# Last step of a blocked state-space scan in four pieces of eight channel groups, with the output matmuls one piece behind

## The chip, the cores and the metric

The kernel runs on one core of a Trainium2 chip. The metric is the device time of one execution in microseconds (us). Five engines matter here: TensorE (PE in the rows, with its weight loads as PEld), VectorE (DVE), ScalarE (ACT), GpSimd (POOL) and SyncE (SP), whose queue issues nearly all transfers.

## The reference, cut to what matters

One inference step of a two-layer backbone. Each layer runs four mixers side by side on 640 tokens (128 prompt tokens and 512 latent tokens): three kinds of attention and one state-space mixer. The change touches only the state-space mixer, which for each of two directions, 32 channel groups and 64 complex states computes a linear recurrence over time and then maps the states to outputs:

```python
bu = jnp.einsum('btgn,gpn->btgp', u, bbar)            # input to the states
_, hs = lax.associative_scan(_lin_combine, (a, bu))   # h[t] = abar * h[t-1] + bu[t], complex
y = jnp.real(jnp.einsum('btgp,gnp->btgn', hs, cmat))  # outputs, per channel group
```

The gate and merge projections of the other branches (`h @ w_in`) have nothing to do with the scan, and the kernel uses them as filling.

## The kernel before, in words

Tokens are cut into 80 chunks of eight. The state at a chunk's edge is what the scan computes; inside a chunk everything is matmuls. The states lie in a tile `H` of 128 partitions by 82 slots by 64 columns: partitions 0 to 63 hold real parts and 64 to 127 imaginary parts of the 64 states, slots are chunk edges, and the 64 columns are 2 directions by 32 channel groups.

`ssm_scan` works on `H` with DVE alone. One complex multiply-add is the helper `madd` (five instructions, L595 to L599): two of 64 partitions each that fetch the imaginary parts for the real rows and the reverse, then three of all 128 partitions. It runs in three levels over blocks of eight chunks: a sequential pass inside blocks (seven steps, tiles `sc1v`, `sc2v`), a sequential pass over the blocks' ends (tiles `sc1c`, `sc2c`), and a last step that spreads the carry of each block to its seven inner slots. The last step is one `madd` per direction over 7 blocks by 7 slots by 32 groups (1568 elements a partition, tiles `sc1f`, `sc2f`), and a small one per direction for the prompt's second block (224 elements, `sc1g`, `sc2g`). The scheduler puts the small ones between the carry steps, since nothing holds them back.

`ssm_out` then makes the outputs in four pieces of eight groups. Each piece loads two tiles of constants (`M`, from `fd`, eight transfers, two buffers; `WY`, from `yd`, two transfers, four buffers) and has two halves; a half is four groups of three matmuls into one PSUM tile `sm` (L645 from `M`, L646 with `H` of direction 0, L647 with `H` of direction 1) and one eviction by ACT (L649).

PE's instructions stand in the order in which the code emits them. Other engines are ordered by a scheduler. Between the steps of the scan the code calls `fill(n)`, which emits the next n units of a queue of gate and merge projections; a unit is three matmuls of 320 columns (L152, L154, L156). So PE has work while DVE scans. The numbers of units are in the table `FILL`: 9 after each inner step, 4 after each carry step, 20 after each large last step, 4 after each small one, and 4 after the scan; one more follows each half of the outputs. After the scan and the outputs come transposes (L1413), GELU and the gated linear unit of the state-space branch, and then the attentions, which go on taking units from the same queue.

Of the kernel before, what the change touches and what calls it, by code (L numbers as in the profile page):

```python
# [15 lines left out]
ALU = mybir.AluOpType  # L16
AX = mybir.AxisListType

P = 128
# [20 lines left out]
GB = 2  # L40
QB, KB, VB, OB = 2, 3, 2, 2

FILL = {"a": 1, "s": 8, "t": 4, "e": 3, "m": 6, "ms": 6, "scan": (9, 4, 20), "l": (8, 8), "f": 0.7, "d": 8, "p": (3, 2), "g": 34}
HD_SCALE = 64 ** -0.5


# [9 lines left out]
def hybrid_kernel(ctx: ExitStack, tc: tile.TileContext, A, O, dbg=None):  # L56
    nc = tc.nc
    V, S, G, T = nc.vector, nc.scalar, nc.gpsimd, nc.tensor
# [12 lines left out]
    def taker(pool):  # L71
        def take(tag, shape, bufs=1, dt=F32):
            return pool.tile(shape, dt, tag=tag, name=nm(tag), bufs=bufs)
        return take
# [6 lines left out]
    def load(dst, src):  # L81
        nc.sync.dma_start(dst, src)
        return dst

    def dump(name, ap, l=None):
        if dbg is not None and f"{name}{l}" in dbg:
            nc.sync.dma_start(dbg[f"{name}{l}"], ap)
# [28 lines left out]
    def psum1():  # L116
        return ps.tile([P, 512], F32, tag="sm", name=nm("sm"), bufs=2)
# [40 lines left out]
    def fm_tile(src, mhi, mlo, nk=KD, eng=V):  # L158

        o = psum2()  # L160
        kc = min(nk, 4)
        for kq in range(nk // kc):
            w = w_chunk(src[kq], [P, kc, P], eng)
            for kk in range(kc):
                k = kq * kc + kk
                mm3([o[:, 0, 192:512], o[:, 1, 0:320]], w[0][:, kk], w[1][:, kk],
                    [mhi[:, k, 0:HF], mhi[:, k, HF:NT]], [mlo[:, k, 0:HF], mlo[:, k, HF:NT]], k == 0, k == nk - 1)
        return run2(o)[:, 192:832]
# [371 lines left out]
    def chunk_powers(l, at):  # L540

        A8, tm = at("A8p", [P, 8, 2, 64]), at("pwt", [P, 4, 64])
        V.tensor_copy(A8[:, 0], A8s[l])
        for n in (1, 2, 4):
            double(A8, n - 1, tm, n)
        V.tensor_scalar(A8[:, :, 1], A8[:, :, 1], sgn, None, op0=ALU.mult)
        return A8
# [31 lines left out]
        V.memset(H[:, 80, 32:64], 0.0)  # L579
        return U  # L580

    def hview(H, rows, d, off, *dims):

        b = H[rows, 1 + off:2 + off, 32 * d:32 * d + 1]
        slot, dg = H.ap[1][0], H.ap[2][0]
        return bass.AP(tensor=b.tensor, offset=b.offset, ap=[b.ap[0]] + [[32 * d_ * dg + s_ * slot, n] for d_, s_, n in dims] + [[dg, 32]])

    def ssm_scan(at, A8, H, final):

        all_, top, bot = slice(0, P), slice(0, 64), slice(64, P)  # L590

        def madd(ar, ai, src, dst, shape, t, nb=1):

            m, m2 = at("sc1" + t, shape, nb), at("sc2" + t, shape, nb)
            V.tensor_tensor(m2[top], ai[bot], src(bot), ALU.mult)  # L595
            V.tensor_tensor(m2[bot], ai[top], src(top), ALU.mult)  # L596
            V.tensor_tensor(m, ar, src(all_), ALU.mult)
            V.tensor_tensor(m2, m2, dst, ALU.add)
            V.tensor_tensor(dst, m, m2, ALU.add)  # L599

        def power(k, n=None):

            for ri in range(2):
                v = A8[:, k - 1, ri].rearrange("p (d g) -> p d g", d=2)
                yield v.unsqueeze(2).to_broadcast([P, 2, n, 32]) if n else v

        for i in range(7):
            ar, ai = power(1, 10)
            v = lambda f, b: (lambda r: hview(H, r, 0, f, (1, b - f, 2), (0, 8, 10)))
            madd(ar, ai, v(i, 7 - i), v(i + 1, 6 - i)(all_), [P, 2, 10, 32], "v")  # L610
            fill(FILL["scan"][0])
        for j in range(1, 8):

            n = 2 if j == 4 else None
            ar, ai = power(8, n)
            both = [(0, 40, 2)] if n else []
            v = lambda f, b: (lambda r: hview(H, r, 0, f, (1, b - f, 2), *both))
            madd(ar, ai, v(8 * j - 1, 64 - 8 * j), v(8 * j + 7, 56 - 8 * j)(all_), [P, 2, 2, 32] if n else [P, 2, 32], "c", 2)
            fill(FILL["scan"][1])
        ar, ai = power(1)  # L620
        madd(ar, ai, lambda r: hview(H, r, 0, 79, (1, -15, 2)), final.rearrange("p (d g) -> p d g", d=2), [P, 2, 32], "c", 2)
        for n in (7, 1):
            for d in range(2):

                sh = [P, n, 7, 32]
                f_, t_ = ((8, 7) if d == 0 else (1, 8)) if n == 7 else ((72, 71) if d == 0 else (65, 72))
                k = slice(0, 7) if d == 0 else slice(6, None, -1)
                ar, ai = (A8[:, k, ri, 32 * d:32 * d + 32].unsqueeze(1).to_broadcast(sh) for ri in range(2))
                madd(ar, ai, lambda r: hview(H, r, d, t_, (0, 8, n), (0, 0, 7)), hview(H, all_, d, f_, (0, 8, n), (0, 1, 7)), sh, "f" if n == 7 else "g")
                fill(FILL["scan"][2] if n == 7 else 4)  # L630

    def ssm_out(l, at, U, H, ysb):

        for gb in range(4):
            g0 = 8 * gb
            M = at("M", [P, 8, P], 2)
            for j in range(8):
                load(M[16 * j:16 * j + 16], fd[l][:, g0:g0 + 8, 16 * j:16 * j + P])
            Y = [load(at("WY", [P, 8, 8, 16], 4), yd[l][2 * gb + d][:, :, 1 - d:9 - d]) for d in range(2)]
            for q in range(2):  # L640
                py = psum1()
                for n in range(4):
                    g = 4 * q + n
                    o = py[0:80, P * n:P * n + P]
                    T.matmul(o, lhsT=U[:, g0 + g], rhs=M[:, g], start=True, stop=False)  # L645
                    T.matmul(o, lhsT=H[:, 1:81, g0 + g], rhs=Y[0][:, g], start=False, stop=False)  # L646
                    T.matmul(o, lhsT=H[:, 1:81, 32 + g0 + g], rhs=Y[1][:, g], start=False, stop=True)  # L647
                a = 16 * (g0 + 4 * q)
                S.activation(ysb[:, :, a:a + 64].rearrange("c i (g n) -> c g i n", g=4),  # L649
                             py[0:80].rearrange("c (g i n) -> c g i n", g=4, i=8), AF.Copy)  # L650
                fill(1)


    queue, owed, emitted, TAIL = [], [0], set(), object()

    def fill(n):

        owed[0] += n
        while owed[0] >= 1 and queue:
            try:  # L660
                next(queue[0])
                owed[0] -= 1
            except StopIteration:
                queue.pop(0)
        owed[0] %= 1
# [11 lines left out]
    def drain(*gens):  # L677
        for g in gens:
            for _ in g:
                pass  # L680
# [112 lines left out]
    def softmax(at, s, p_out, scale, total):  # L793

        mx = at("mx", [P, 2], 6)
        V.tensor_reduce(mx[:, 0:1], s, axis=AX.X, op=ALU.max, negate=True)  # L796
        if scale is None:
            S.activation(p_out, s, AF.Exp, bias=mx[:, 0:1], accum_out=total)
        else:
            V.tensor_tensor(mx[:, 1:2], mx[:, 0:1], scale, ALU.mult)  # L800
            S.activation(p_out, s, AF.Exp, bias=mx[:, 1:2], scale=scale, accum_out=total)
# [32 lines left out]
    def slot():  # L834

        due = [fn for n, fn in later if n == 0]
        later[:] = [(n - 1, fn) for n, fn in later if n > 0]
        for fn in due:
            fn()
# [4 lines left out]
    def p_t(at, p, pp, fl=1.0):  # L844

        out = []
        for k0, nk in ((0, 2), (2, 2), (4, 1)):
            if k0 == 4:
                fill(fl * 2)
                slot()  # L850
                fill(fl * (FILL["t"] - 2))
            pt = psum1()
# [11 lines left out]
            if w == 384:  # L864
                out.append((hi[:, 256:384], lo[:, 256:384]))
        fill(fl * FILL["e"])
        return out
# [14 lines left out]
    def attend64(at, passes, v, scale, o, row, total, done=None, fl=1.0):  # L882
# [12 lines left out]
        for half in range(2):  # L895
            p, pp = at("p", [P, 2, NT], PB), at("pp", [P, P], 2) if half else None
            for jj in range(2):
# [3 lines left out]
                if j == 3:  # L901
                    softmax(at, s[1], pp, scale(4), total[:, 4, row // 64:row // 64 + 1])
            fill(fl * FILL["a"])
            slot()
# [410 lines left out]
    for l in range(DEPTH):  # L1315
# [10 lines left out]
        for k in range(KD):  # L1326
            sh, sc = mods[l, 0], mods[l, 1]
            t = xat("ht", [P, NT], 2)
# [53 lines left out]
        at = taker(sp)  # L1382
# [13 lines left out]
        H, final = at("H", [P, 82, 64]), at("final", [P, 64])  # L1396
        A8 = chunk_powers(l, at)
        U = ssm_states(l, at, ucm, H, final)
        ssm_scan(at, A8, H, final)
        fill(4)  # L1400
        dump("H", H, l)
        ysb = at("cm", [80, 8, 512])
        ssm_out(l, at, U, H, ysb)
        dump("ysb", ysb, l)

        yh = at("U", [P, 4, NT])
# [38 lines left out]
        at = lambda tag, *a, takers=(taker(bp), taker(kp)): takers[tag in ("k", "q", "v")](tag, *a)  # L1445
# [8 lines left out]
        b = []  # L1454
# [22 lines left out]
        for d_ in range(KD):  # L1477
            bo = fm_tile(A["wbo"][l, 1, d_], *b, 4, G)
            t = load(xat("ht", [P, NT], 2), ttd[l][1][d_])
# [7 lines left out]
        for d_ in range(KD):  # L1487
            g = fm_tile(A["wout"][l, d_], mhi, mlo, KD, G)
# [184 lines left out]
```

## Time and profile before

| what | before |
|---|---|
| median of 3 runs | 2258.31 us (2257.4 to 2258.47) |
| the profiled execution's own time | 2259.87 us |
| its span, first to last instruction | 2258.1 us |
| PE busy | 2069.8 us, 92% |
| DVE busy | 1333.8 us, 59% |
| ACT busy | 965.6 us, 43% |
| POOL busy | 795.5 us, 35% |
| mean granted TensorE clock | 0.959 of full |

Times inside the trace count from the start of the span. The state-space mixer of layer 0 ends its scan near 467 us, that of layer 1 near 1567 us. A wait is the idle time of an engine in front of an instruction, put down to the instruction that released it.

### The profile page before, as it was taken

The numbers are of one execution on the slowest core, as the hardware profiler recorded it, in microseconds if no ns is written. First come the engines' busy times: TensorE is split into PE (matmuls) and PEld (weight loads), VectorE is DVE, ScalarE is ACT, GpSimd is POOL, SyncE is SP. The second block draws the span as 40 slices with busy tenths as digits, with TensorE's granted clock in tenths as the row PEclk, the third lists the DMA queues.
The fourth block names the chain that finished last, engine by engine and source line by source line (L and its number), as shares of the span: only waits on it lengthen the run. The fifth ranks groups of instructions, "written<-read, shape, count | busy, mean of one in ns | idle before, by whom it ended". The sixth has DMA issues, their size and how long they took to land. (4 is left out here: it accounts for less than half of the span.)

```text
span 2258.1 us, 38400 instructions
## 1 busy us (share of the span) xinstructions
PE 2069.8 (92%) x14389; PEld 1993.9 (88%) x14389; DVE 1333.8 (59%) x2461; ACT 965.6 (43%) x1972; POOL 795.5 (35%) x561
## 2 busy tenths in 40 slices
PE   5888899969999999998798999997899999999997
PEld 3787789969998899998787999997899899999997
DVE  7899372935544455664877774367445445566542
ACT  3342344324554455553233434341455455555332
POOL 1655432403311232345563364232142223234522
PEclk9889899989999999999898999998999999999998
DMA  7366675535555665666573577653474445666653
GB/s 253 101 233 212 202 268 160 154 76 187 177 155 158 189 198 167 183 197 194 178 258 116 150 246 240 206 186 88 120 242 135 147 134 156 185 187 188 203 156 112
DMA packets 240538, 400.62 MB, mean 177 GB/s; under 512 B 37536, under 2 KB 112288, under 8 KB 240352
## 3 DMA queue, kind: packets, MB, share of 16 engines
q1 hardware_dynamic: 226112, 372.14, 53.9%
q10 hardware_dynamic: 14240, 26.02, 3.1%
q8 instruction: 113, 1.85, 0.4%
q14 instruction: 73, 0.60, 0.1%
HBM read 279.68 MB, written 117.87 MB: 176 GB/s over the span
## 5 line engine op out<-in xcount | busy, mean ns | idle before, releaser
L135 POOL TENSOR_TENSOR flo<-fraw,fhi 128x512 fp32r<-128x512 f32 x304 | 436.2, 1439 | 937.9 <-ACT fhi L134 854.6
L152 PE MATMUL mm<-hhi,fhi 128*128 128x320 f32 x2048 | 669.9, 327 | 22.8 <-DVE gt L774 8.2
L156 PE MATMUL mm<-hhi,flo 128*128 128x320 f32 x2048 | 642.5, 314 | 4.3 <-POOL flo L135 4.3
L154 PE MATMUL mm<-hlo,fhi 128*128 128x320 f32 x2048 | 641.6, 313 | 0.0
L152 PEld LDWEIGHTS mm<-hhi,fhi 128*128 128x128 f32 x2048 | 394.7, 193 | 38.2 <-issue 7.6
L156 PEld LDWEIGHTS mm<-hhi,flo 128*128 128x128 f32 x2048 | 392.7, 192 | 5.4 <-POOL flo L135 5.4
L154 PEld LDWEIGHTS mm<-hlo,fhi 128*128 128x128 f32 x2048 | 394.5, 193 | 0.4
L134 ACT ACTIVATE fhi<-fraw 128x512 fp32r<-128x512 f32 x304 | 190.1, 628 | 128.6 <-PE mm L154 94.5
L135 DVE TENSOR_TENSOR ptl<-sm,pth 128x512 fp32r<-128x512 f32 (+1 forms) x240 | 142.2, 620 | 171.7 <-ACT pth L134 171.4
L796 DVE TENSOR_REDUCE mx<-s 128x1 f32<-128x640 f32 (+1 forms) x240 | 167.5, 714 | 112.3 <-PE s L829 57.7
L135 POOL TENSOR_TENSOR wlo<-wraw,whi 128x512 fp32r<-128x512 f32 (+1 forms) x80 | 114.6, 1436 | 231.4 <-ACT whi L134 224.7
L134 ACT ACTIVATE pth<-sm 128x512 fp32r<-128x512 f32 (+1 forms) x240 | 122.3, 543 | 163.5 <-PE sm L856 126.6
L829 PE MATMUL s<-k,q 128*128 128x384 f32 (+5 forms) x1008 | 158.4, 304 | 1.7 <-DMA q<-gqd 1.1
L829 PEld LDWEIGHTS s<-k,q 128*128 128x128 f32 (+1 forms) x1008 | 154.7, 189 | 2.5 <-issue 1.6
L152 PE MATMUL mm<-bh,fhi 128*128 128x320 f32 x384 | 126.4, 329 | 6.5 <-DVE gt L774 3.2
L134 ACT ACTIVATE whi<-wraw 128x512 fp32r<-128x512 f32 (+1 forms) x96 | 59.2, 618 | 170.7 <-PE s L154 90.6
L856 PE MATMUL sm<-ident,p 128*128 128x128 f32 x800 | 116.1, 274 | 5.3 <-DVE ptl L135 3.2
L879 PE MATMUL sm<-pth,v 128*128 128x256 f32 (+1 forms) x528 | 120.2, 282 | 0.0
L727 ACT ACTIVATE gt<-mm 128x320 f32<-128x320 f32 x192 | 82.9, 432 | 86.9 <-PE mm L156 84.9
L156 PE MATMUL mm<-bh,flo 128*128 128x320 f32 x384 | 119.5, 311 | 0.0
L154 PE MATMUL mm<-bl,fhi 128*128 128x320 f32 x384 | 119.3, 311 | 0.0
L879 PE MATMUL sm<-ptl,v 128*128 128x256 f32 (+1 forms) x440 | 112.5, 281 | 0.0
(418 smaller groups left out, 3995.6 us busy)
## 6 DMA issues: line engine op xcount, KB each, us to landing
fraw<-in_wmerge SPq DMA_DIRECT2D x128, 256.0 KB, 3.0
fraw<-in_wgate SPq DMA_DIRECT2D x64, 256.0 KB, 2.9
mgd<-gt SPq DMA_DIRECT2D x48, 320.0 KB, 2.9
fraw<-in_wbo SPq DMA_DIRECT2D x48, 256.0 KB, 2.9
k<-dkd SPq DMA_DIRECT2D x64, 192.0 KB, 4.1
gtd<-gt SPq DMA_DIRECT2D x32, 320.0 KB, 3.2
pv<-mgd SPq DMA_DIRECT2D x32, 320.0 KB, 3.7
pv<-brd SPq DMA_DIRECT2D x30, 320.0 KB, 3.7
```

The lines of the kernel that those rows point to most:

```text
L134: S.activation(hi, src, AF.Copy)
L135: eng.tensor_tensor(lo, src, f(hi), ALU.subtract)
L152: T.matmul(outs[i], lhsT=whi, rhs=mhis[i], start=first, stop=False)
L154: T.matmul(outs[i], lhsT=whi, rhs=mlos[i], start=False, stop=False)
L156: T.matmul(outs[i], lhsT=wlo, rhs=mhis[i], start=False, stop=last)
L727: S.activation(t[:, r[0]], r[1], AF.Tanh, scale=0.5)
L796: V.tensor_reduce(mx[:, 0:1], s, axis=AX.X, op=ALU.max, negate=True)
L829: T.matmul(o, lhsT=tok(q, t), rhs=k[:, a:b], start=i == 0, stop=i == n - 1)
L856: T.transpose(pt[:, a:a + P], p[:, jj, P * kt:P * kt + P], ident)
L879: T.matmul(o, lhsT=v, rhs=p_, start=n == 0, stop=n == len(todo) - 1)
```

## The change

The last step is turned round. First the two small steps of the prompt are emitted. Then the carries of the seven blocks (both directions, all groups) are copied once into a tile `sw` with real and imaginary parts exchanged, by two copies of 64 partitions. With that tile a multiply-add needs four instructions, all of 128 partitions. The last step is cut into four pieces of eight channel groups; a piece does both directions (2 times 4 instructions of 7 by 7 by 8, that is 392 elements). `ssm_scan` and `ssm_out` become generators, and the caller takes them in turn: after the second, third and fourth piece of the scan the outputs of the piece before it are emitted, and the last outputs follow the scan. The units of filling: 4 after each small step, 29 after the first piece, 5 after each of the other three.

```diff
-FILL = {..., "scan": (9, 4, 20), ...}
+FILL = {..., "scan": (9, 4, 29, 5), ...}
...
-        for n in (7, 1):
+
+        sw = at("sw", [P, 2, 7, 32])
+        for to, of in ((top, bot), (bot, top)):
+            V.tensor_copy(sw[to], hview(H, of, 0, 7, (1, 1, 2), (0, 8, 7)))
+        for d in range(2):
+            f_, t_ = (72, 71) if d == 0 else (65, 72)
+            ...
+            madd(ar, ai, lambda r: hview(H, r, d, t_, (0, 0, 7)), hview(H, all_, d, f_, (0, 1, 7)), [P, 7, 32], "g")
+            fill(4)
+        for g in range(0, 32, 8):
             for d in range(2):
-                sh = [P, n, 7, 32]
-                ...
-                madd(ar, ai, ..., sh, "f" if n == 7 else "g")
-                fill(FILL["scan"][2] if n == 7 else 4)
+                f_, t_ = (8, 7) if d == 0 else (1, 8)
+                sh = [P, 7, 7, 8]
+                ...
+                V.tensor_tensor(m2, ai, sw[:, d, :, g:g + 8].unsqueeze(2).to_broadcast(sh), ALU.mult)
+                V.tensor_tensor(m, ar, hview(H, all_, d, t_, (0, 8, 7), (0, 0, 7), g=g, ng=8), ALU.mult)
+                V.tensor_tensor(m2, dst_, m2, ALU.subtract)
+                V.tensor_tensor(dst_, m, m2, ALU.add)
+            fill(FILL["scan"][3 if g else 2])
+            yield
...
                 fill(1)
+            yield
...
-        ssm_scan(at, A8, H, final)
+        ysb = at("cm", [80, 8, 512])
+        out = ssm_out(l, at, U, H, ysb)
+        for i, _ in enumerate(ssm_scan(at, A8, H, final)):
+            if i:
+                next(out)
         fill(4)
+        drain(out)
         dump("H", H, l)
-        ysb = at("cm", [80, 8, 512])
-        ssm_out(l, at, U, H, ysb)
```

The lines that are matmuls L645, L646, L647 before are L663, L664, L665 in the changed kernel.

First place: DVE, the last step of layer 0's scan. In the kernel before:

```order
L595 TENSOR_TENSOR sc2f_4321<-A8p_3562,H_3560 64x1568
L599 TENSOR_TENSOR final_3561<-sc1c_4313,sc2c_4314 128x64
L596 TENSOR_TENSOR sc2f_4321<-A8p_3562,H_3560 64x1568
L597 TENSOR_TENSOR sc1f_4320<-A8p_3562,H_3560 128x1568
L598 TENSOR_TENSOR sc2f_4321<-sc2f_4321,H_3560 128x1568
L599 TENSOR_TENSOR H_3560<-sc1f_4320,sc2f_4321 128x7x7x32
L595 TENSOR_TENSOR sc2f_4406<-A8p_3562,H_3560 64x1568
L596 TENSOR_TENSOR sc2f_4406<-A8p_3562,H_3560 64x1568
L597 TENSOR_TENSOR sc1f_4405<-A8p_3562,H_3560 128x1568
L598 TENSOR_TENSOR sc2f_4406<-sc2f_4406,H_3560 128x1568
L599 TENSOR_TENSOR H_3560<-sc1f_4405,sc2f_4406 128x7x7x32
```

And in the changed kernel at the same place, up to the first piece's two writes of `H` (`final` is the small result of the last carry step):

```order
L627 COPY sw_4321<-H_3560 64x448
L601 TENSOR_TENSOR final_3561<-sc1c_4314,sc2c_4315 128x64
L627 COPY sw_4321<-H_3560 64x448
L644 TENSOR_TENSOR sc1f_4378<-A8p_3562,H_3560 128x392
L643 TENSOR_TENSOR sc2f_4379<-A8p_3562,sw_4321 128x392
L643 TENSOR_TENSOR sc2f_4385<-A8p_3562,sw_4321 128x392
L645 TENSOR_TENSOR sc2f_4379<-H_3560,sc2f_4379 128x392
L644 TENSOR_TENSOR sc1f_4384<-A8p_3562,H_3560 128x392
L646 TENSOR_TENSOR H_3560<-sc1f_4378,sc2f_4379 128x7x7x8
L645 TENSOR_TENSOR sc2f_4385<-H_3560,sc2f_4385 128x392
L643 TENSOR_TENSOR sc2f_4499<-A8p_3562,sw_4321 128x392
L646 TENSOR_TENSOR H_3560<-sc1f_4384,sc2f_4385 128x7x7x8
```

The ten instructions of 1568 elements (of which the last writes direction 1 for all groups) became two copies and 32 instructions of 392; the sixth and the ninth of them write the first eight groups of direction 0 and of direction 1.

Second place: PE in layer 0, from the end of the outputs' first piece to the start of the second. Before, one unit of filling stands there:

```order
L647 MATMUL sm_4590<-WY_4570,H_3560 80x128
L152 MATMUL mm_4618<-hhi_283,fhi_4608 128x320
L154 MATMUL mm_4618<-hlo_284,fhi_4608 128x320
L156 MATMUL mm_4618<-hhi_283,flo_4609 128x320
L645 MATMUL sm_4635<-M_4622,U_3584 80x128
```

In the changed kernel six units stand there, two on one PSUM tile and four on the next (the left-out rows repeat those above them):

```order
L665 MATMUL sm_4570<-WY_4551,H_3560 80x128
L152 MATMUL mm_4524<-hhi_283,fhi_4520 128x320
L154 MATMUL mm_4524<-hlo_284,fhi_4520 128x320
L156 MATMUL mm_4524<-hhi_283,flo_4521 128x320
...
L152 MATMUL mm_4603<-hhi_283,fhi_4514 128x320
L154 MATMUL mm_4603<-hlo_284,fhi_4514 128x320
L156 MATMUL mm_4603<-hhi_283,flo_4515 128x320
...
L663 MATMUL sm_4629<-M_4616,U_3584 80x128
```

Ahead of the first output matmul, ten units fewer stand after the carry steps than before (42 in place of 52). Five units each moved to between the first and second and the second and third piece, and four stand ahead of the fourth. In all the scan's end and the outputs take 64 units from the queue in place of 60.

## Rows read from the trace of the kernel before

**Rows 1.** PE's waits over the whole run: total us, times, longest.
```profile
PE sm L647 <- DVE H L599: 16.5, 2, 8.3
PE sm L646 <- DVE H L599: 13.8, 2, 7.2
...
PE mm L152 <- DVE gt L774: 11.4, 11, 3.6
...
PE sm L647 <- DMA WY<-yd: 3.9, 2, 2.2
...
PE sm L646 <- DMA WY<-yd: 1.2, 2, 0.9
```

**Rows 2.** Timeline of layer 0's last step: start, length, engine [idle before].
```profile
448.45 1.79 DVE L595 TENSOR_TENSOR sc2f<-A8p,H 64x1568 f32<-64x1568 f32 x1
...
451.57 0.38 PE L645 MATMUL sm<-M,U 128*80 128x128 f32 x2
458.63 0.72 PE L646 MATMUL sm<-WY,H 128*80 128x128 f32 x2 [6.67 <-DVE H L599]
...
467.60 0.71 PE L647 MATMUL sm<-WY,H 128*80 128x128 f32 x2 [8.25 <-DVE H L599]
```

**Rows 3.** Timeline of layer 1's last step.
```profile
1547.55 1.79 DVE L595 TENSOR_TENSOR sc2f<-A8p,H 64x1568 f32<-64x1568 f32 x1
...
1550.18 0.38 PE L645 MATMUL sm<-M,U 128*80 128x128 f32 x2
...
1564.85 1.79 DVE L599 TENSOR_TENSOR H<-sc1f,sc2f 128x1568 f32<-128x1568 f32 x1
1566.70 0.72 PE L647 MATMUL sm<-WY,H 128*80 128x128 f32 x2 [8.25 <-DVE H L599]
```

**Rows 4.** DVE's instructions by line: count, shortest/median/longest ns, first and last start.
```profile
L596 DVE TENSOR_TENSOR sc2g<-A8p,H x4: 385/386/386, 433.9 to 1539.8; 64x224 f32<-64x224 f32 x4
L596 DVE TENSOR_TENSOR sc2f<-A8p,H x4: 1784/1785/1786, 450.5 to 1559.5; 64x1568 f32<-64x1568 f32 x4
...
L474 DVE TENSOR_TENSOR WY<-PW,BB x16: 1209/1213/2532, 74.3 to 1147.5; 128x1024 f32<-128x1024 f32 x16
...
L543 DVE COPY A8p<-A x2: 219/220/221, 329.5 to 1428.6; 128x128 f32<-128x128 f32 x2
```

**Rows 5.** Timeline of DVE in layer 1's carry steps.
```profile
1541.01 0.22 DVE L596 TENSOR_TENSOR sc2c<-A8p,H 64x64 f32<-64x64 f32 x1
1541.26 0.23 DVE L597 TENSOR_TENSOR sc1c<-A8p,H 128x64 f32<-128x64 f32 x1
1541.40 0.22 DVE L598 TENSOR_TENSOR sc2c<-sc2c,H 128x64 f32<-128x64 f32 x1
```

**Rows 6.** Timeline of POOL around layer 1's last step.
```profile
1549.67 2.83 POOL L135 TENSOR_TENSOR flo<-fraw,fhi 128x512 fp32r<-128x512 f32 x1 [3.97 <-ACT fhi L134]
```

**Rows 7.** Timeline of PE: first matmuls of two units of filling that follow each other.
```profile
1605.36 0.30 PE L152 MATMUL mm<-hhi,fhi 128*128 128x320 f32 x1
...
1605.79 0.31 PE L152 MATMUL mm<-hhi,fhi 128*128 128x320 f32 x1
```

**Rows 8.** Timeline of layer 1's outputs: SP's loads, PE's pieces, the transposes.
```profile
1573.96 4.39 SPq L82 DMA_DIRECT2D M<-fd  x8
1578.45 1.25 SPq L82 DMA_DIRECT2D WY<-yd  x2
...
1574.49 0.38 PE L645 MATMUL sm<-M,U 128*80 128x128 f32 x2
...
1581.55 0.38 PE L645 MATMUL sm<-M,U 128*80 128x128 f32 x2
...
1585.11 0.54 PE L647 MATMUL sm<-WY,H 128*80 128x128 f32 x2 [1.71 <-DMA WY<-yd]
...
1600.21 0.72 PE L1413 MATMUL s<-ident,cm 80*128 80x80 f32 x8
```

**Rows 9.** Busy time by stretch, layer 1's outputs: PE busy, granted clock, DMA.
```profile
1586.80:1590.20 3.40, 3.40 (x17) 0.50 0.96 262
```

More of the change, by code (lines that the diff above doesn't have):

```diff
@@ L41 @@
 QB, KB, VB, OB = 2, 3, 2, 2
-FILL = {"a": 1, "s": 8, "t": 4, "e": 3, "m": 6, "ms": 6, "scan": (9, 4, 20), "l": (8, 8), "f": 0.7, "d": 8, "p": (3, 2), "g": 34}
+FILL = {"a": 1, "s": 8, "t": 4, "e": 3, "m": 6, "ms": 6, "scan": (9, 4, 29, 5), "l": (8, 8), "f": 0.7, "d": 8, "p": (3, 2), "g": 34}
 HD_SCALE = 64 ** -0.5
@@ L580, in ssm_states, with hview @@
         return U
-    def hview(H, rows, d, off, *dims):
-        b = H[rows, 1 + off:2 + off, 32 * d:32 * d + 1]
+    def hview(H, rows, d, off, *dims, g=0, ng=32):
+        b = H[rows, 1 + off:2 + off, 32 * d + g:32 * d + g + 1]
         slot, dg = H.ap[1][0], H.ap[2][0]
-        return bass.AP(tensor=b.tensor, offset=b.offset, ap=[b.ap[0]] + [[32 * d_ * dg + s_ * slot, n] for d_, s_, n in dims] + [[dg, 32]])
+        return bass.AP(tensor=b.tensor, offset=b.offset, ap=[b.ap[0]] + [[32 * d_ * dg + s_ * slot, n] for d_, s_, n in dims] + [[dg, ng]])
     def ssm_scan(at, A8, H, final):
@@ L621, in ssm_scan @@
         madd(ar, ai, lambda r: hview(H, r, 0, 79, (1, -15, 2)), final.rearrange("p (d g) -> p d g", d=2), [P, 2, 32], "c", 2)
-        for n in (7, 1):
+        sw = at("sw", [P, 2, 7, 32])
[3 more added lines that the diff above has]
+            f_, t_ = (72, 71) if d == 0 else (65, 72)
+            k = slice(0, 7) if d == 0 else slice(6, None, -1)
+            ar, ai = (A8[:, k, ri, 32 * d:32 * d + 32] for ri in range(2))
+            madd(ar, ai, lambda r: hview(H, r, d, t_, (0, 0, 7)), hview(H, all_, d, f_, (0, 1, 7)), [P, 7, 32], "g")
+            fill(4)
+        for g in range(0, 32, 8):
             for d in range(2):
-                sh = [P, n, 7, 32]
-                f_, t_ = ((8, 7) if d == 0 else (1, 8)) if n == 7 else ((72, 71) if d == 0 else (65, 72))
+                f_, t_ = (8, 7) if d == 0 else (1, 8)
                 k = slice(0, 7) if d == 0 else slice(6, None, -1)
-                ar, ai = (A8[:, k, ri, 32 * d:32 * d + 32].unsqueeze(1).to_broadcast(sh) for ri in range(2))
-                madd(ar, ai, lambda r: hview(H, r, d, t_, (0, 8, n), (0, 0, 7)), hview(H, all_, d, f_, (0, 8, n), (0, 1, 7)), sh, "f" if n == 7 else "g")
-                fill(FILL["scan"][2] if n == 7 else 4)
+                sh = [P, 7, 7, 8]
+                ar, ai = (A8[:, k, ri, 32 * d + g:32 * d + g + 8].unsqueeze(1).to_broadcast(sh) for ri in range(2))
+                m, m2 = at("sc1f", sh, 2), at("sc2f", sh, 2)
+                dst_ = hview(H, all_, d, f_, (0, 8, 7), (0, 1, 7), g=g, ng=8)
+                V.tensor_tensor(m2, ai, sw[:, d, :, g:g + 8].unsqueeze(2).to_broadcast(sh), ALU.mult)
[4 more added lines that the diff above has]
+            yield
     def ssm_out(l, at, U, H, ysb):
```

## The prediction

> **What bounds the kernel now.** I read the page first: PE is busy 92% of the span (the table above), so only stretches in which PE stands still have something to give. PE's own waits, largest first, show where: apart from one wait at the start, the two largest are those of the outputs' first matmuls for the scan's last writes of `H`, 16.5 us for direction 1 and 13.8 us for direction 0, two times each, once a layer [rows 1]. The timelines of the two places show how they arise [rows 2, 3]. DVE begins the last step at 448.45 (layer 0) and 1547.55 (layer 1). PE has used up its 52 units of filling by 451.57 and 1550.18, does the one matmul that needs no `H`, and waits; direction 0 comes at 458.63, direction 1 at 467.60 and 1566.70. In layer 0 PE stands still 6.67 + 8.25 us. The reader is to see that DVE is the late one: it works without a gap on ten instructions of 1.8 us, and the first output of the first group waits for the last write of the thirty-second. A smaller wait follows: in the third piece of the outputs PE waits for the loads `WY`, 3.9 + 1.2 us over both layers [rows 1].
>
> **The change, part by part.** All times count from S, the start of the last step.
>
> *DVE's path to the first eight groups.* Ahead of the narrow instructions stand two copies and the small `final` addition. No copy of 64 by 448 is in the trace. A product of 64 by 224 takes 386 ns and one of 64 by 1568 1785 ns, so a line of 1.041 ns per element on 153 ns [rows 4]; at that rate a copy of 448 costs 0.62 us, the upper bound. The copy of 128 elements takes 220 ns, where the line says 286, which is what two elements per step would give; so the lower bound is 153 + 233 = 0.39 us [rows 4]. I take 0.39, since the row at hand is a copy. With gaps the two copies and the addition cost 0.41 + 0.24 + 0.41 = 1.06 us (1.52 at the upper bound).
>
> A narrow instruction of 392 elements is 153 + 408 = 0.56 us by the line. What counts is the distance between starts. The row at 1541.26, of all 128 partitions, lasts 0.23 us, and the next starts 0.14 later, so two such instructions overlap by some 0.08 to 0.09; the half-height one before it is followed only after 0.25, its length and a little more [rows 5]. The 32 narrow ones are all full height, and by the order none waits for the one just before it (the nearest is two before). So I take 0.56 - 0.08 = 0.48 us a step; the upper bound is 0.585, no overlap. The ninth writes direction 1 of the first groups: 8 x 0.48 + 0.56 = 4.40 us. A matmul starts 0.06 after the write it waits for (1564.85 + 1.79 = 1566.64, and 1566.70) [rows 3]. PE passes at S + 1.06 + 4.40 + 0.06 = S + 5.52: 453.97 and 1553.07, where before it was 467.60 and 1566.70. That is **13.63 us earlier**. By the wait values in the built program each piece of outputs waits for the writes of its own eight groups, not for the whole tile. The POOL split that held DVE up once before (2.83 us from 1549.67) [rows 6] followed units that now come after this point, and the one before it ended at 1549.67 - 3.97 = 1545.70, before S [rows 6].
>
> *Filling.* Ten units fewer stand ahead of the outputs. A unit takes 1605.79 - 1605.36 = 0.44 us [rows 7], so **4.4 us** of PE's work come back later. PE arrives 4.4 us earlier, and stands still about 6.2 us in layer 0 and 6.7 in layer 1. Net per layer 13.63 - 4.4 = **9.23 us**. The four units by which 64 exceeds 60 are work taken from later slots and cost nothing by themselves.
>
> *Pieces two to four.* A piece of outputs takes 1581.55 - 1574.49 = 7.06 us with two units in it [rows 8], and now has five (the last: four) more in front. DVE needs 8 x 0.48 = 3.84 us a piece, against 7.06 + 2.2 = 9.3 of PE, so it stays ahead; even at 0.585 a step it does. The narrow instructions of pieces two to four therefore lie beside PE's work and cost nothing; if that cover were gone (each longer than 1.1 us), they would be the bound.
>
> *Loads of the third and fourth piece.* They wait for buffers that the first piece gives back. In layer 1 the eight `M` issues start at 1573.96 and take 4.39 us, the two `WY` follow, and the second is there when PE goes on at 1585.11, that is 11.15 us after the release [rows 8]. Before, the third piece followed 1581.55 - 1573.96 = 7.6 us after the release. Now 0.44 + 2.2 + 7.06 + 2.2 = 11.9 us lie between. So this wait goes: **5.1 us** over both layers [rows 1]. For the fourth piece it is 11.4 us against the same 11.15, tight, but I take nothing for it; both ends are 0 and 5.1. On SP's queue two fewer weight loads stand ahead of these loads, and the one that now stands behind them is needed some 11 us after the outputs end, so nothing is late there.
>
> *The clock.* From 1586.80 to 1590.20, just after that load wait in layer 1, the granted clock was 0.50, which is 1.2 GHz, and PE worked all 3.40 us [rows 9]. Without the wait this may not recur; at full clock half of it, 1.7 us, would be left over. Layer 0 had the same wait and no such dip near it, so I leave it out of the sum and give it to the lower end.
>
> **Sum.** 2 x 9.23 + 5.1 = 23.6 us. The profiled execution took 2259.87 (its span 2258.1 and 1.8 around it), so 2236.3; it was 1.56 above the median of the runs shown, 2258.31, which makes **2234.8**, said as 2235.
>
> *A rule against the change.* The row shows an overlap of 0.08 us between full-height instructions [rows 5]. The Trainium skill, VectorE: DVE Perf Modes, section "The DRAIN you can't avoid", says that after every instruction the pipeline empties before the next begins, and the section on the TRN2 errata asks for 512 elements or more, because each instruction pays a fixed latency. The change goes from 1568 to 392. By that rule the sum is the rival "no overlap" below; by the row it is the one above. The row, being this kernel's, decides, though it is a 64-element one.
>
> **The rivals.**
> - *No overlap.* Each narrow step takes 0.585 and each copy 0.62: 8 x 0.105 + 0.46 = 1.3 us a layer, **2237.4**. For it: the overlap rests on short rows. Against: full-height rows start 0.14 apart.
> - *Narrow runs at half rate.* Rows of eight elements cost twice: 0.97 us in place of 0.56, steps 0.41 longer: 9 x 0.41 = 3.7 a layer, **2242**. Against: 1024 elements read in pieces (eight groups by eight powers) take 1213 ns, the line says 1219 [rows 4].
> - *Loads still late.* Heavier traffic, and the third piece waits as before: **2239.9**. The margin is 0.7 us.
> - *Given back.* PE reaches the GELU and the attentions earlier, and they do not follow: a half gives 2246.5, all of it 2258. Against: the waits of PE are on its own products or on engines that it feeds; a fixed clock is nowhere. The units shift by four against everything that follows, so waits such as those for `gt` (11.4 us in 11 places, the longest 3.6) may come or go [rows 1]: 3.6 us to either side.
> - *It waits for the whole tile.* If the first output had to wait for all four pieces, PE would pass at S + 1.06 + 31 x 0.48 + 0.62 = S + 16.6, 2.6 us earlier than before and with 4.4 us of filling to make up: 1.8 lost a layer and the 5.1 won, **2257**. Against: the wait values.
> - *Slower.* Each run of eight costs a restart in the narrow instructions (49 runs each). Then DVE paces the outputs. They end, by the sum above, 42.6 us after S; before the transposes followed at 1600.21, or S + 52.66 [rows 8], and with the four units more 54.4 is the break-even. The last write must come 7.5 us before that: 1.06 + 32 p = 46.9, so p = 1.43 us, or 19 ns a run. At 25 ns a run p is 1.70, the outputs end at S + 63, 8.7 us late a layer: **2276**. Against: the same row of 1213 ns, with 64 runs and no sign of it.
>
> **How the numbers follow.** The forecast has 0.62, no overlap 0.10, half rate 0.04, loads 0.08, half given back 0.06, wholly given back 0.04, whole tile 0.02, slower 0.04. A change under 0.2% (4.5 us) is about what a measurement of this kernel cannot tell from none. The first five cases lie below 2253.8: faster 0.90; wholly given back and whole tile are 0.06; slower 0.04. The low end is the sum less the dip (1.7) and less 3.6 of shifted waits, 2229.5, said as 2229. The high end takes the loads (5.1), no overlap (2.6) and 3.6, 2246, and reaches to half given back: 2248. What is left out is about 0.10 above and 0.08 below.
>
> **What would show it right or wrong.** In the changed kernel's trace: PE's wait for direction 0 and 1 of the first piece should be 5 to 7 us together a layer, and there should be none for `H` in the other pieces; starts of narrow DVE instructions 0.48 apart; the two copies 0.39 each; the first direction-1 matmul 5.5 us after the first copy; no wait of PE for `WY`; and from there all stages about 12 us (layer 1: 23.6) earlier. It is wrong if a narrow instruction takes 1 us or more, if PE waits in the second or third piece, or if the attentions' stretch grows by what was won.

## The result, and the profile after

The changed kernel takes 2230.77 us (median of 4 runs, 2229.54 to 2231.95). Beside it the kernel before took 2258.39. The ratio is 0.987, 95% interval 0.9855 to 0.9885: 27.6 us less, where 23.3 were forecast (2235). The profiled execution took 2231.81, its span 2230.0; it is the one the rows below come from.

First the page: span, and busy time of each engine.

```profile
span 2230.0 us, 38443 instructions
PE 2063.6 (93%) x14389; PEld 1988.4 (89%) x14389; DVE 1326.4 (59%) x2509; ACT 963.5 (43%) x1972; POOL 781.1 (35%) x561
```

The span is 28.1 us shorter (2258.1 before). PE's busy time is 6.2 us shorter (2069.8 before), with the same 14389 matmuls; PE's idle time, span less busy, went from 188.3 to 166.4, 21.9 us less. These two parts have different causes, and only the second was forecast. PE's waits, total us, times, longest:

```profile
PE sm L664 <- DVE H L646: 10.7, 2, 5.7
...
PE mm L152 <- DVE gt L793: 6.0, 5, 4.4
...
PE sm L665 <- DMA WY<-yd: 2.5, 2, 1.3
...
PE sm L665 <- DVE H L646: 1.4, 2, 0.7
...
PE sm L664 <- DMA WY<-yd: 0.4, 1, 0.4
```

Against [rows 1]: for `H` 30.3 us became 12.1, for `WY` 5.1 became 2.9. That is 20.4 of the 21.9 us; the waits for `gt` (the tile that takes the filling's products) fell by another 7.4 us, and others rose by nearly as much. The timeline of layer 0's last step shows where the first comes from (start, length; rows 2 and 3 have the same place before):

```profile
446.69 0.38 PE L663 MATMUL sm<-M,U 128*80 128x128 f32 x2
...
447.97 0.39 DVE L627 COPY sw<-H 64x448 f32<-64x448 f32 x1
448.37 0.23 DVE L601 TENSOR_TENSOR final<-sc1c,sc2c 128x64 f32<-128x64 f32 x1
448.61 0.39 DVE L627 COPY sw<-H 64x448 f32<-64x448 f32 x1
449.03 0.57 DVE L644 TENSOR_TENSOR sc1f<-A8p,H 128x392 f32<-128x392 f32 x1
449.51 1.04 DVE L643 TENSOR_TENSOR sc2f<-A8p,sw 128x392 f32<-128x392 f32 x2
...
451.42 0.56 DVE L646 TENSOR_TENSOR H<-sc1f,sc2f 128x392 f32<-128x392 f32 x1
451.90 0.56 DVE L645 TENSOR_TENSOR sc2f<-H,sc2f 128x392 f32<-128x392 f32 x1
452.03 0.72 PE L664 MATMUL sm<-WY,H 128*80 128x128 f32 x2 [4.97 <-DVE H L646]
452.37 0.56 DVE L643 TENSOR_TENSOR sc2f<-A8p,sw 128x392 f32<-128x392 f32 x1
452.85 0.56 DVE L646 TENSOR_TENSOR H<-sc1f,sc2f 128x392 f32<-128x392 f32 x1
...
453.46 0.72 PE L665 MATMUL sm<-WY,H 128*80 128x128 f32 x2 [0.71 <-DVE H L646]
```

S is 447.97. The copies and the addition are over at S + 1.06, the narrow instructions start 0.48 apart and last 0.56, and PE passes direction 1 at S + 5.49. In layer 1 the wait for `WY` is seen best (SP's queue, then PE):

```profile
1557.42 6.67 SPq L82 DMA_DIRECT2D M<-fd  x8
1564.21 1.23 SPq L82 DMA_DIRECT2D WY<-yd  x2
...
1571.15 0.51 PE L665 MATMUL sm<-WY,H 128*80 128x128 f32 x2 [1.27 <-DMA WY<-yd]
```

This is the fourth piece; the third does not wait. SP's own waits, over the whole run, have a row that bears on it:

```profile
SPq L82 <- DMA ttd<-gt: 6.4, 2, 3.2
```

These are the fourth piece's `M` issues, once a layer: one of the eight stands 3.2 us (in layer 1 until 1562.35), by the trace until the store `ttd<-gt` of a filling product has landed, which ACT issues at 1560.18.

### The profile page after: what moved, and what is told of

It reads as the page before. It is cut to its first block, busy times and chain, and to the rows that moved or that the text cites. A ratio compares the mean times of both kernels' runs of the same rounds, so it can differ in the third digit from the quotient of the medians.

```text
span 2230.0 us, 38443 instructions
## 1 busy us (share of the span) xinstructions
PE 2063.6 (93%) x14389; PEld 1988.4 (89%) x14389; DVE 1326.4 (59%) x2509; ACT 963.5 (43%) x1972; POOL 781.1 (35%) x561
## 5 line engine op out<-in xcount | busy, mean ns | idle before, releaser
L135 POOL TENSOR_TENSOR flo<-fraw,fhi 128x512 fp32r<-128x512 f32 x304 | 423.3, 1396 | 926.7 <-ACT fhi L134 838.6
L875 PE MATMUL sm<-ident,p 128*128 128x128 f32 x800 | 116.4, 274 | 11.5 <-DVE ptl L135 4.4
```

The costliest lines, as they stand in the source:

```text
L135: eng.tensor_tensor(lo, src, f(hi), ALU.subtract)
L875: T.transpose(pt[:, a:a + P], p[:, jj, P * kt:P * kt + P], ident)
```

## The experiments

| kernel | ratio to before (95%) | span | PE busy | PE idle | wait for `H` | for `WY`, `M` | for `gt` |
|---|---|---|---|---|---|---|---|
| before | 1 | 2258.1 | 2069.8 | 188.3 | 30.3 | 5.1 | 21.2 |
| changed | 0.987 (0.9855 to 0.9885) | 2230.0 | 2063.6 | 166.4 | 12.1 | 2.9 | 13.8 |
| e1 four units back | 0.9876 (0.9863 to 0.989) | 2229.4 | 2063.3 | 166.1 | 12.8 | 2.3 | 19.2 |
| e2 outputs behind | 0.9847 (0.983 to 0.9863) | 2220.6 | 2062.9 | 157.7 | 5.2 | 4.0 | 13.6 |
| e3 pieces alone | 0.9862 (0.9848 to 0.9875) | 2232.0 | 2062.4 | 169.6 | 14.2 | 2.1 | 14.0 |
| e4 exchange alone | 0.9965 (0.9952 to 0.9978) | 2257.5 | 2067.9 | 189.6 | 25.1 | 5.0 | 21.0 |
| e5 62 units | 0.9795 (0.9778 to 0.9811) | 2206.2 | 2056.7 | 149.5 | 0.3 | 3.6 | 6.1 |
| e6 `WY` first | 0.9844 (0.9827 to 0.986) | 2219.1 | 2060.9 | 158.2 | 5.0 | 2.8 | 13.2 |
| e7 splits on DVE | 0.9906 (0.989 to 0.9922) | 2235.5 | 2064.5 | 171.0 | 0 | 4.2 | 13.8 |
| e8 four groups first | 0.984 (0.9825 to 0.9856) | 2221.5 | 2064.0 | 157.5 | 1.7 | 6.3 | 13.8 |
| e9 three `M` buffers | 0.9849 (0.9828 to 0.987) | 2231.2 | 2067.6 | 163.6 | 0 | 0 | 22.0 |
| e10 before, 86 units | 0.9862 (0.9848 to 0.9875) | 2225.5 | 2065.5 | 160.0 | 0 | 5.5 | 21.9 |
| e11 68 units | 0.9836 (0.9823 to 0.985) | 2218.7 | 2059.7 | 159.0 | 0 | 16.1 | 11.5 |
| e12 62, `WY` first | 0.9797 (0.9781 to 0.9812) | 2208.7 | 2056.3 | 152.4 | 0.3 | 3.1 | 6.9 |

The waits are sums of the rows of PE's waits in one profiled execution each; the ratios are over 4 to 6 runs each. An execution's own time lies up to 8.5 us from its kernel's median (e9 has the widest spread, 2216.9 to 2233.0), so a row is read for its waits and the ratio for the time.

**Which half of the change gains: e3 and e4.** e3 has the pieces without the exchanged copy, e4 the copy and the four-instruction form at full width.

```diff
-        sw = at("sw", [P, 2, 7, 32])
-        ...
-                V.tensor_tensor(m2, ai, sw[:, d, :, g:g + 8]..., ALU.mult)
-                ...
+                madd(ar, ai, lambda r: hview(H, r, d, t_, ..., g=g, ng=8), hview(H, all_, d, f_, ..., g=g, ng=8), sh, "f", 2)
```

> The changed kernel without the copy of the carries with re and im exchanged: each piece uses the old five-instruction multiply-add (ten instructions of 64 or 128 partitions a piece in place of eight). Theory (the gain is from the pieces): without the copies the pieces begin 0.8 us earlier and the last write of the first eight groups comes some 9 x 0.5 + 0.6 + 0.3 for half-height ones that do not overlap = 5.6 us after the small final addition's place, so PE's wait for H stays 5 to 7 us a layer and the time is that of the changed kernel, 2230.8 to 2232. Rival (the exchange is what gains, through four instructions in place of five): PE waits 2 us or more longer a layer, 2235 or more.

```diff
-FILL = {..., "scan": (9, 4, 29, 5), ...}
+FILL = {..., "scan": (9, 4, 20), ...}
...
-        for g in range(0, 32, 8):
+        for g in range(0, 32, 32):
...
-                sh = [P, 7, 7, 8]
+                sh = [P, 7, 7, 32]
...
-            fill(FILL["scan"][3 if g else 2])
-            yield
+                fill(FILL["scan"][2])
+        yield
...
-        for i, _ in enumerate(ssm_scan(at, A8, H, final)):
-            if i:
-                next(out)
+        drain(ssm_scan(at, A8, H, final))
```

> The other half alone: copies with re and im exchanged and the four-instruction multiply-add, but at full width (32 groups, 1568 elements), with 20 units behind each direction and the outputs behind the whole step, as before the change. Theory (the gain is from the pieces): the last write comes 1.06 + 7 x 1.70 + 1.79 = 14.8 us after the step's start, where it was 19.1; about 4.3 us less wait a layer, 2249 to 2251. Rival (the exchange is the main gain): 2238 or less. By the forecast's terms both halves together do not add up, since with pieces only the first eight instructions count.

e3: 2228.46, ratio 0.9862, not told from the changed kernel; PE waits 1.05 us longer a layer for `H`, half of what the rival needed. e4: 2252.93 beside 2260.22, 0.9965. So the pieces are nearly the whole gain, and the exchange by itself is worth about a quarter of it and next to nothing on top of the pieces. The exchange was expected to save 4.3 us a layer and saved 2.6 (30.3 to 25.1): in each layer one of its eight wide instructions (of 1568 elements), the one of line 643 at 452.18 and at 1553.16, lasts 2.86 and 2.85 us beside a split of weights on POOL, in place of 1.79. That is 1.1 of the 1.7 us a layer that are missing. (A split takes the raw weights of the filling, `fraw`, and makes a high part `fhi`, on ACT, and a rest `flo`, here on POOL, before PE can use them.)

**Is the interleaving needed: e2.**

```diff
-        for i, _ in enumerate(ssm_scan(at, A8, H, final)):
-            if i:
-                next(out)
+        drain(ssm_scan(at, A8, H, final))
```

> The changed kernel, but all four pieces of the outputs behind the whole last step, as before the change; the same units, now 56 of them ahead of the first output in place of 42. Theory: the gain is that PE waits for eight groups only and that DVE is faster; interleaving by itself is not needed. PE comes 14 x 0.44 = 6.2 us later, so the wait for H falls from 6.4 to 0.3 us a layer; no units stand between the pieces, so the third piece waits for its WY loads as before (2.6 us a layer, where it is 1.5 now): 2 x (6.1 - 1.1) = 10 us faster, about 2221. Rival: the outputs between the groups are what gains (loads hidden, PE fed while DVE works); then it is slower than the changed kernel, 2236 and up.

2224.9, ratio 0.9847: 5 us below the changed kernel by the ratios (the intervals overlap by a little), so the rival falls: interleaving by itself gains nothing; the 14 units that it places between the pieces are worth at least as much in front of them. But 5.2 us of wait for `H` are left where 0.6 were expected. The timeline of its last step, DVE and POOL:

```profile
451.61 2.14 DVE L643 TENSOR_TENSOR sc2f<-A8p,sw 128x392 f32<-128x392 f32 x2
453.68 0.55 DVE L645 TENSOR_TENSOR sc2f<-H,sc2f 128x392 f32<-128x392 f32 x1
454.15 1.62 DVE L644 TENSOR_TENSOR sc1f<-A8p,H 128x392 f32<-128x392 f32 x1
...
451.95 1.38 POOL L135 TENSOR_TENSOR flo<-fraw,fhi 128x512 fp32r<-128x512 f32 x1 [3.98 <-ACT fhi L134]
453.71 1.64 POOL L135 TENSOR_TENSOR flo<-fraw,fhi 128x512 fp32r<-128x512 f32 x1 [0.39 <-ACT fhi L134]
```

The row of two (x2) lasts 1.04 in the changed kernel and 2.14 here, the other 0.56 and 1.62: a DVE instruction that meets one of POOL's splits takes 1.1 us longer. The added units need two more split weights, and both splits fall into DVE's path to the first eight groups: 2 x 1.1 a layer, 4.4 of the missing 4.6 us. The Trainium skill, SBUF — State Buffer, section "SBUF: two separate sides", says that VectorE and GpSimd share a pair of ports, which whoever starts first has for its whole instruction. The rows agree.

**More units, and how many: e5, e11, e10.**

```diff
-FILL = {..., "scan": (9, 4, 29, 5), ...}
+FILL = {..., "scan": (9, 4, 29, 7), ...}
```

> The kernel with the outputs behind the whole last step (e2), with seven units in place of five after each of the second to fourth piece: 62 units ahead of the first output in place of 56. In e2 PE still waits for H 1.7 + 0.9 us a layer, where 0.3 was expected: two splits of weights on POOL, for the units added, fall among DVE's first narrow instructions, and each such instruction lasts 1.1 us longer (2.14 and 1.62 us). Theory: the wait left is simply covered by six units more (2.6 us): no wait for H, 5 us less than e2, about 2220. Rival 1: the units bring another pair of splits among DVE's first eleven instructions, DVE is 2.1 us later, and some 2 us of wait a layer stay: 2224. Rival 2: the units are missed later, where they covered other waits: the wait goes, the time does not.

> The kernel with 62 units ahead of the outputs (e5) with six units more (nine in place of seven after each of the second to fourth piece). Theory: e5 had no wait for H left, so six units more change nothing there; they only come from later: the time of e5, 2212, give or take 2. Rival: e5 was 6 us better than its waits explain because more units ahead of the outputs put the attentions in a better place of the queue; then six more move it again, by 3 us or more to either side.

e5 (62 units): 2211.95, ratio 0.9795. The wait for `H` is gone, with the two splits still inside DVE's path, so rival 1 falls; the time fell with the wait, so rival 2 falls too. Against e2 it is 0.0052 of 2258, 11.7 us, where the wait for `H` explains 4.9; what made the other 7 no run isolates. The span is 14.4 us shorter, 8.2 of it idle (waits for `gt` fell too, by 7.5, and others rose) and 6.2 PE's busy time. In e11 (nine in place of seven, 68 units) the time goes back to 2221.32, 0.9836: not "the time of e5, give or take 2" and more than the 3 us of the rival, and the rows show a cause that the rival did not name. These are its rows, PE's largest new wait, then POOL, DVE, SP and PE:

```profile
PE sm L663 <- DMA M<-fd: 7.8, 2, 3.9
...
457.15 11.92 POOL L135 TENSOR_TENSOR flo<-fraw,fhi 128x512 fp32r<-128x512 f32 x2 [3.60 <-ACT fhi L134]
...
466.41 1.52 DVE L646 TENSOR_TENSOR H<-sc1f,sc2f 128x392 f32<-128x392 f32 x1
...
467.54 1.89 SPq L82 DMA_DIRECT2D fraw<-in_wgate  x2
469.52 4.49 SPq L82 DMA_DIRECT2D M<-fd  x8
...
475.83 0.69 PE L663 MATMUL sm<-M,U 128*80 128x128 f32 x2 [3.87 <-DMA M<-fd]
```

The two splits are merged into one row; the longer takes 10.36 us, from 457.15 to 467.51, while DVE issues narrow instructions 0.48 apart. Only the last narrow instruction, at 466.41, which starts after the one before it has ended and not 0.08 us sooner, is stretched, and POOL gets through; in layer 1 the same row is again 11.92 long. The raw weights' buffer comes free, SP issues the two weight loads that stand ahead of `M` (467.54), `M` follows at 469.52, and PE waits 3.87. So POOL, too, can be held, here over nineteen narrow instructions. It does not happen to every split: two others in the same run of DVE (450.12 and 451.88) took 1.38 and 1.68 us. What decides was not traced.

e10 goes back to the kernel before:

```diff
-FILL = {..., "scan": (9, 4, 20), ...}
+FILL = {..., "scan": (9, 4, 37), ...}
```

> The kernel before, with nothing changed but the units of filling: 37 in place of 20 after each direction of the last step, 34 more ahead of the first output (86). Theory A: what costs is only that PE stands still for H, 14.9 us a layer, and units in its place are as good as a faster DVE; each unit is 0.44 us, so 34 cover 15 us, but every pair of splits for the units added falls among DVE's instructions and costs it 2.2 us, so 3 to 5 us of wait a layer stay: 30 - 8 = 22 us less, and some us from the clock, about 2233, near the changed kernel. Theory B (the units are missed later): 34 units a layer taken from the attentions let PE wait there instead; no more than 10 us faster, 2248. If A holds, the pieces are worth only what the units they save are worth later, and e5 (2212) shows that as the difference.

This kernel before with 34 units more ahead of the outputs and nothing else: 2227.31, ratio 0.9862, and the changed kernel's interval (0.9855 to 0.9885) holds it. Theory B falls. What the change gains over before can be had by filling alone. The price shows in the rows: six of DVE's ten wide instructions in layer 0 last 2.8 us, and DVE's `gt` work for the units stands behind the scan, so PE waits for it in place of `H` (timeline, DVE and PE):

```profile
454.47 2.87 DVE L598 TENSOR_TENSOR sc2f<-sc2f,H 128x1568 f32<-128x1568 f32 x1
...
472.10 0.88 DVE L737 SCALAR_TENSOR_TENSOR gt<-gt,mm 128x320 f32<-128x320 f32 x2
...
472.63 0.63 PE L152 MATMUL mm<-hhi,fhi 128*128 128x320 f32 x1 [6.90 <-DVE gt L737]
```

In layer 1 it is the same (7.76 us). The pieces with the best of three numbers of units (e5) are 15 us below that; on the kernel before only this one number was tried, so what the pieces are worth beside its best filling is not known.

**The loads: e6, e9, e12.** e6 puts the two `WY` loads of a piece ahead of its `M` loads in e2; e9 gives `M` three buffers in e5; e12 is e5 with `WY` first.

```diff
+            Y = [load(at("WY", ...), ...) for d in range(2)]
             M = at("M", [P, 8, P], 2)
             for j in range(8):
                 load(M[16 * j:16 * j + 16], ...)
-            Y = [load(at("WY", ...), ...) for d in range(2)]
```

> The kernel with the outputs behind the whole last step (e2), with the two WY loads of a piece issued ahead of its eight M loads. In e2 the third piece waits 1.8 us a layer for WY: the M issues take 3.7 us of SP's queue first (464.94 to 468.58), WY follows at 468.68. Theory: it is the place in SP's queue that makes WY late: WY is issued 3.7 us earlier and its wait goes, M is issued 1.2 us later and lands just in time: 3 to 4 us less than e2, about 2221.5. Rival: the transfers are what takes the time, not the queue; then M comes late instead, by 1 to 2 us a layer, and nothing is gained.

e6: 2222.19, 0.9844, no change that can be told from e2. The wait for `WY` (4.0) is gone and PE waits 2.8 us for `M` instead: the rival held.

```diff
-            M = at("M", [P, 8, P], 2)
+            M = at("M", [P, 8, P], 3)
```

> The kernel with 62 units ahead of the outputs (e5), with three buffers for M in place of two. In e5 PE waits for nothing but WY in the outputs, 1.8 us a layer in the third piece, because the M loads of that piece stand ahead of WY in SP's queue and wait for the first piece's buffer. Theory: with a third buffer the eight M loads of the third piece go out before the step ends, only WY waits for the first piece, and is issued some 3.3 us earlier: the wait goes, 3.6 us less than e5, about 2208 (ratio to before 0.978). Rival: the wait moves to the fourth piece, whose M then waits for the first piece's buffer and stands behind: 2211 to 2212.

e9: 2224.68, 0.9849, slower than e5 by 12 us, though PE waits for no load and no `H` in the outputs any more. Neither theory saw why. The timeline of SP, DVE and ACT shows it:

```profile
425.00 0.33 SPq L82 DMA_DIRECT2D fraw<-in_wmerge  x1
441.56 1.06 SPq L82 DMA_DIRECT2D wraw<-in_wglu  x2
442.72 6.58 SPq L82 DMA_DIRECT2D fraw<-in_wmerge  x4
...
440.85 0.68 DVE L135 TENSOR_TENSOR wlo<-wraw,whi 128x512 fp32r<-128x512 f32 x1
...
446.62 1.30 ACT L134 ACTIVATE fhi<-fraw 128x512 fp32r<-128x512 f32 x2 [12.14 <-DMA fraw<-in_wmerge]
```

SP issues nothing from 425.3 to 441.56. The load it holds then is of the next stage's weights (`wraw`), whose buffer comes free with DVE's split `wlo`, which ends at 441.53. With the third buffer the scheduler had moved that split behind most of the carry steps on DVE; in e5 it stands ahead of them (the first of two at 411.0). The filling's weights stand behind on SP, come late, and PE stands still 7.25 us at 448.30, ahead of the outputs.

> The kernel with 62 units ahead of the outputs (e5) and the WY loads issued ahead of the M loads (e6), which changes the order on SP's queue alone. Theory: the wait for H stays zero, as in e5; the 3.6 us of wait for WY become some 2.8 of wait for M, as in e6: the time of e5 less 1, 2210 to 2212 (ratio to before 0.979). Rival: e5's time hung on where its loads happened to fall; with other loads first the time is 2218 or more, as with 68 units or with three M buffers.

e12: 2213.13, 0.9797. e5's time came again with other loads first, so the rival falls. With e5 it is the fastest version tried: 46 us below before, 17 below the changed kernel.

**The splits on DVE: e7.** `V` is DVE and `G` is POOL; `LAST[0]` is true from the start of the last step to its end.

```diff
...
-        ws = ws or [w_chunk(src[kq], [P, kc, P], G, "f") for kq in range(nk // kc)]
+        ws = ws or [w_chunk(src[kq], [P, kc, P], V if LAST[0] else G, "f") for kq in range(nk // kc)]
```

> The kernel with the outputs behind the whole last step (e2), with the splits of weights that are emitted in the last step done by DVE itself in place of POOL. DVE does a split of 128 by 512 in 0.69 us; one on POOL takes 1.3 us and makes the DVE instruction beside it 1.1 us longer. Theory (POOL's split holds DVE): no narrow instruction over 0.6 us but where a split stands; DVE's path to the first piece has 2 x 0.6 in place of 2 x 1.1 us: PE's wait for H falls by 0.9 us a layer, about 1 to 2 us in all, 2223. Rival (the long instructions have another cause): they stay long, DVE has the splits on top, and PE waits 1.2 us more a layer, 2227.

e7: 2234.76, 0.9906, slower, and not for the rival's reason. The narrow instructions of the first piece are all 0.56 long, so POOL's split is what stretched them in e2. But the splits now stand in DVE's order behind the carry steps, and PE waits for them:

```profile
PE mm L157 <- DVE flo L136: 15.3, 2, 8.0
```

**Shorter still: e8.** The first piece in two of four groups.

```diff
-        for g in range(0, 32, 8):
+        for g, n in ((0, 4), (4, 4), (8, 8), (16, 8), (24, 8)):
...
```

> The kernel with the outputs behind the whole last step (e2), with the first eight groups done in two pieces of four (instructions of 196 elements), so that the first half of an output piece can start on four groups. Theory (starts of full-height instructions lie 0.08 us closer than their length, whatever the length): length 153 + 204 = 0.36 us, starts 0.28 apart, direction 1 of four groups written at 1.06 + 7 x 0.28 + 0.36 = 3.4 us, where eight take 5.5: PE's wait for H falls from 2.6 to 0.5 us a layer, 4 us less than e2, about 2221. Rival (a floor per instruction near 0.45): starts 0.45 apart, first write at 4.7, 0.8 us less a layer, about 2223.5.

```profile
454.43 0.35 DVE L644 TENSOR_TENSOR sc1f<-A8p,H 128x196 f32<-128x196 f32 x1
454.71 0.35 DVE L645 TENSOR_TENSOR sc2f<-H,sc2f 128x196 f32<-128x196 f32 x1
```

196 elements last 0.35 us and start 0.27 to 0.28 apart: the line of [rows 4] and the overlap of 0.08 hold there too. The wait for `H` falls from 5.2 to 1.7, and 2.3 of that come back as wait for `WY`: 2221.27, 0.984, not told from e2.

**Where the excess is from: e1.**

```diff
-            fill(8)
+            fill(7)
```

> The changed kernel with seven units of filling in place of eight at each of the four calls of the GELU loop, so that the attentions start at the same place of the unit queue as in the kernel before (the four units that the change emits more, ahead of the outputs, are taken back in the next stage). Theory: some 4 us of the 27.6 us come from this shift of four units, which took away waits of PE for gt in the attentions (6.0 us in 5 places, where before it was 11.4 in 11). Then the waits for gt come back to about 11 us and the time is 2234 to 2236. Rival: the shift is worth nothing and the excess over the forecast comes from somewhere else (the granted clock, the rest of the loads); then it is 2230.8, give or take 1, with waits for gt near 6.

e1: 2232.59, 0.9876. The waits for `gt` of line 793 came back as the theory says (10.8 us in 11 places), and the time did not: 0.0006 of the ratio is 1.4 us and within the intervals. The theory is not borne out: in the profiled executions the shift of four units moves waits about without changing their sum (idle 166.1 and 166.4). The times alone would still leave room for its lower end, some 3 us.

## Why the prediction was right, and where it was not

The path that the forecast is built on held in each term. That the total came out within 4.3 us is in part luck: the loads gave 2.9 us less than forecast, and a term that the sum lacked gave more than that back.

- **DVE's path** held in each term: copies and addition 1.06, narrow steps 0.48, PE past direction 1 at S + 5.49 (forecast 5.52). The rivals "no overlap", "half rate" and "slower" are out by these rows, "whole tile" by the first `L664` at 452.03, when 25 of the 32 narrow instructions had not begun. The Trainium skill's rule that was weighed (each instruction waits until the pipeline is empty) does not hold for these: 0.56 long, 0.48 apart. The same page of the Trainium skill, section "Two Vector instructions with no wait between them", has the exception that fits: an instruction that is not held starts while the one before still runs.
- **PE's wait left** was to be 6.2 and 6.7 us: 5.68 and 6.41. For `H` 18.2 us went, where 2 x 9.23 = 18.5 were forecast. No other piece waits for `H`. Two slips of the working cost nothing: the two starts of [rows 7] lie 0.43 us apart, not 0.44, and of the ten wide instructions one in each layer lasts 2.74 us, not 1.8.
- **The loads** are the step that was mis-sized: 5.1 us were to go, 2.2 went, and the sign "no wait of PE for `WY`" failed. The third piece is clear as forecast. The term took nothing for the fourth (11.4 us between release and use, against 11.15 for the loads). In layer 1 the use came 11.8 us after the release (1569.22 less 1557.42), but the loads took 13.7: the eight `M` issues 6.67 us in place of the 3.65 of the third piece, and `WY`, issued from 1564.21, was there at 1571.15. The difference is SP's wait of 3.2 us for the store of a filling product. All three kernels with five units between the pieces (changed, e1, e3) have it in both layers; in e2 and e5, which have only the one unit after each half, it is absent, and the eight issues take 3.6 to 4.0 us. So the units that were to hide the loads brought a store that held them up. Why a load stands behind this store is not shown.
- **What the sum lacked** made up for it: PE's busy time, 6.2 us shorter for the same matmuls, of which 1.7 had been named and left out. The windows (length, then busy time of PE, PEld, DVE, ACT, POOL, the granted clock, DMA share, GB/s) of before show stretches at 1.2 GHz inside full work:

```profile
525.00:530.00 5.00, 5.00 (x26) 5.00 (x25) 2.34 (x3) 1.32 (x2) 0.00 (x0) 0.66 0.44 146
985.00:990.00 5.00, 5.00 (x26) 4.96 (x26) 1.68 (x8) 2.31 (x5) 3.45 (x3) 0.66 0.72 243
...
2070.00:2075.00 5.00, 5.00 (x20) 4.96 (x21) 2.16 (x13) 1.01 (x2) 2.00 (x2) 0.51 0.59 170
```

  These are gone after the change, as is that of [rows 9]. Half of the time at that clock is lost: 1.7 + 1.7 + 2.4 us in these three. The changed kernel has its own, of 1.7 us each at 545 to 550 and 1160 to 1165, and others behind PE's waits in the scan:

```profile
455.00:460.00 5.00, 5.00 (x34) 5.00 (x33) 5.00 (x11) 0.59 (x1) 0.00 (x0) 0.78 0.01 3
...
1540.00:1545.00 5.00, 5.00 (x23) 5.00 (x24) 5.00 (x11) 0.51 (x1) 0.00 (x0) 0.50 0.00 0
```

  Summed over the run in stretches of 5 us, busy time times the share of the clock that was withheld is about 56 us before and 51 after (an estimate from such rows), so the clock is most of the 6.2 us. But the waits for `H` have no part in it: behind them the changed kernel lost 2.1 us (450 to 460) and 3.3 (1535 to 1550), the kernel before 1.7 (455 to 475) and 2.0 (1550 to 1570).

  In e5 the same stretch, from the first output to the last of layer 0, is at full clock:

```profile
455.03:481.18 26.15, 24.23 (x183) 23.86 (x181) 11.46 (x24) 4.28 (x8) 1.28 (x1) 1.00 0.56 140
```

  In layer 1 of e5 a dip to 0.74 (1540 to 1545) follows the wait of 1.75 us for `WY`. In e5 and e12, where PE stands 0.3 us for `H`, busy time is another 7 us shorter (2056.7 and 2056.3); but in e7, e9 and e10, which have no wait for `H` and stand some 7 us a layer for something else ahead of the outputs, it is 2064.5 to 2067.6. That a dip follows a standing PE in the scan, and in layer 0 goes with the wait, the rows show. Why dips far from the change went too was only argued: e1, which moved the waits for `gt` back, did not bring the busy time back (2063.3). It stays open.
- "Given back" did not happen: layer 0's attentions took 500.8 us where it was 504.8, layer 1's 495.8 where it was 500.5, with 1.8 us of filling less in each. The sign "about 12 us earlier" came out only late: the transposes of layer 0 start 7.2 us earlier (499.6 and 492.4; the four units more are 1.8 of the difference), its attentions 9.3, and their end 13.2; in layer 1 the transposes are 22.4 us earlier and the end of the attentions 28.6.

## What to carry to other kernels

Where an engine waits for a step that works on the whole tile, count its idle time first, and then both ways to end it: hand over the first piece early, or put more independent work in front. Here the first is this change and the second alone (e10) is worth the same; together (e5) they are worth 46 us. Filling is limited by what it brings with it, here weights to be split on POOL and loaded on SP: 56, 62 and 68 units took 2224.9, 2212.0 and 2221.3 us. A change of a buffer or an engine can reorder a queue far away, so compare the order as well as the numbers (e7, e9).

## What was not expected of the hardware

- A DVE instruction that meets one of POOL's splits (1.3 to 1.7 us beside the narrow ones) lasts 1.1 us longer, at 196, 392 and 1568 elements alike (1.46, 1.62, 2.87 us in place of 0.35, 0.56, 1.79).
- The reverse can be worse: beside DVE's narrow instructions, 0.48 apart without a gap, one split took 10.36 us (e11), where others beside the same run took 1.4 to 1.7.
- Eight load issues on SP's queue took 6.67 us in place of 3.65 when a store of 320 KB was issued from ACT's queue among them; 3.2 us of it were one wait, put down to that store.
- The start of a narrow full-height DVE instruction lies 0.08 us ahead of the end of the one before, at 392 and at 196 elements.
